# Hybrid decoder block, dense expert gates: in every second quad of tokens ScalarE builds the weighted table of first keys by itself

## The chip, the cores and the metric

The kernel runs on one core of one Trainium2 chip. The metric is device time in microseconds (us) of one execution. The engines are named as in the profile: PE is TensorE (PEld its weight loads), DVE is VectorE, ACT is ScalarE, POOL is GpSimd, SP is SyncE. Each engine works through its own instructions in order; engines wait for each other through semaphores.

## The reference, cut to what matters

One decoder layer on 1024 tokens of width 1024: a mixer (sliding-window attention and a gated convolution between an input and an output projection), and then a PEER layer, in which each token picks 128 of 16384 small experts (8 heads, 16 each). An expert's number is idx = e1 * 128 + e2, from two halves of the key search, and each has a gate:

```python
sc, ci = lax.top_k(cand, PEER_TOPK)
e1 = jnp.take_along_axis(i1, ci // PEER_TOPK, axis=-1)
e2 = jnp.take_along_axis(i2, ci % PEER_TOPK, axis=-1)
idx = e1 * N_KEYS + e2
gates = jax.nn.softmax(sc, axis=-1).astype(h.dtype)
...
a = jax.nn.gelu(jnp.einsum('td,thkd->thk', hx, u), approximate=False)
return jnp.einsum('thk,thkd->td', gx * a, vsel)
```

## The kernel before

The 1024 tokens are 8 tiles of 128. Three tiles (2, 6, 7) are "sparse": their experts' rows are gathered from memory one by one (POOL issues the gathers, DVE does the dot products, L970, and the sums, L977). Five tiles (0, 1, 3, 4, 5) are "dense": for them every expert is computed by matrix products (L1122 and L1168), and the result is weighted with a full matrix G of gates, one number for each expert and token, nearly all of them zero.

G is what the change is about. It is made in dense_gates1, one tile after the other, in quads of four tokens (32 quads to a tile, 160 in all; 8 quads fill one staging tile stg, which a DMA then writes to memory as part of G_d). For one token the 128 chosen experts lie on the partitions. Two tables of 128 x 128 are needed: oh2 has a one in each row at the column of e2, and og has the gate in each row at the column of e1. PE multiplies them (L846, four tokens to a quad), which gives the 128 x 128 gates of that token, and ACT copies the four from the PSUM bank G to stg (L847).

Before the change, DVE makes both tables of a quad in one is_equal against the row of numbers 0 to 127 in keyno (L823, 128 x 1024), with ones in both. Then the first one is multiplied with the gates: in quads 2 and 5 of each eight by ACT, token by token (L832, four instructions), in the other six by POOL in one instruction (L836). The tables oh have three buffers, so DVE can begin a quad when PE has done the one three before it.

All this runs beside the rest. The mixer and the key search are a "front" that runs three times (g0: tiles 0 to 2, g1: tiles 3 to 5, g2: tiles 6 and 7): input projection (lin_g1in), attention and convolution, output projection (lin_g1o), norm, query projection and key search (lin_g1q, pkg). Its weights come by DMA (raw), are split by ACT into a high part H (L223) and by POOL into a low part L (L224), and PE multiplies both (L268). The gates of tiles 0 and 1 are made beside front g1, those of tiles 3, 4 and 5 beside front g2, and a first part of the gathers of sparse tile 2 beside both. A counter in the program sets how many quads belong to each step of the front (gates_of.run); what is left by the end of g1's output projection is finished there (gates_of.rest). Up to the end of front g2 the order on each engine is then set by a scheduler at build time, which goes by its own estimates; the order is fixed when the kernel runs. The dense products behind it have an order written out by hand.

In names such as oh_1_40 the first number is the tile and the second the first token of the quad; G1_1_2 is the bank of tile 1, staging tile 1, quad 2. eT and gT hold e1, e2 and the gates of a tile, transposed.

Of the kernel before, what the change touches and what calls it, by code (L numbers as in the profile page):

```python
# [9 lines left out]
F32 = mybir.dt.float32  # L10
# [4 lines left out]
AF = mybir.ActivationFunctionType  # L15
ALU = mybir.AluOpType
PSUM = bass.MemoryType.PSUM

P = 128
# [4 lines left out]
NK = 128  # L24
# [60 lines left out]
def block_kernel(  # L85
# [18 lines left out]
    nc = tc.nc  # L104
# [48 lines left out]
    with ExitStack() as fctx:  # L153
# [14 lines left out]
        def bank(which, name):  # L168
            return (ps_a if which == "a" else ps_t).tile([P, 512], F32, tag="b", name=name)
# [20 lines left out]
        for i in range(7):  # L190
            pt = bank("t", f"selT_ps{i}")
# [6 lines left out]
        iota = fs.tile([P, NK], F32, name="iota")  # L198
        nc.gpsimd.iota(
            iota, pattern=[[1, NK]], base=0, channel_multiplier=0, allow_small_or_imprecise_dtypes=True  # L200
# [601 lines left out]
        def dense_gates(gg, tiles):  # L802
            for i in tiles:
                yield from dense_gates1(gg, i)

        def dense_gates1(gg, i):
            e1, e2 = yield from select(i)
            pt = bank("t", f"eT{i}")
            for k, s in enumerate((e1, e2, gates[i])):
                nc.tensor.transpose(pt[:, k * P : (k + 1) * P], s, ident)  # L810
            eT = gg.tile([P, 2, P], BF16, tag="eT", name=f"eT{i}", bufs=1)
            gT = gg.tile([P, P], F32, tag="gT", name=f"gT{i}", bufs=1)
            nc.scalar.copy(eT.rearrange("p a b -> p (a b)"), pt[:, : 2 * P])
            nc.scalar.copy(gT, pt[:, 2 * P : 3 * P])
            tg0 = DENSE.index(i) * (P // TG)
            pend = []
            for tg in range(P // TG):
                stg = gg.tile([P, NK, TG], F32, tag="stg", name=f"stg{i}_{tg}", bufs=2)
                for q in range(TG // 4):
                    t0 = tg * TG + q * 4  # L820

                    oh = gg.tile([P, 2, 4, NK], F32, tag="oh", name=f"oh_{i}_{t0}", bufs=3)
                    nc.vector.tensor_tensor(  # L823
                        oh,
                        keyno.unsqueeze(1).unsqueeze(1).to_broadcast([P, 2, 4, NK]),
                        eT[:, :, t0 : t0 + 4].unsqueeze(3).to_broadcast([P, 2, 4, NK]),
                        op=ALU.is_equal,
                    )
                    og, oh2 = oh[:, 0], oh[:, 1]
                    if q % 3 == 2:  # L830
                        for k in range(4):
                            nc.scalar.activation(  # L832
                                og[:, k, :], og[:, k, :], AF.Copy, scale=gT[:, t0 + k : t0 + k + 1]
                            )
                    else:
                        nc.gpsimd.tensor_tensor(  # L836
                            og, og, gT[:, t0 : t0 + 4].unsqueeze(2).to_broadcast([P, 4, NK]), op=ALU.mult
                        )
                    if pend:
                        pend.pop()()  # L840

                    def matmuls(oh2=oh2, og=og, stg=stg, tg=tg, q=q):

                        ps = bank("t", f"G{i}_{tg}_{q}").rearrange("p (e t) -> p e t", t=4)
                        for k in range(4):
                            nc.tensor.matmul(ps[:, :, k], oh2[:, k, :], og[:, k, :], start=True, stop=True)  # L846
                        nc.scalar.copy(stg[:, :, q * 4 : q * 4 + 4], ps)  # L847
                        if q == TG // 4 - 1:
                            nc.scalar.dma_start(
                                G_d.rearrange("b p g f -> p g b f")[:, tg0 + tg],  # L850
                                stg.rearrange("p (b e) t -> p b (e t)", e=GB),
                            )

                    pend.append(matmuls)
                    yield 1.2
            pend.pop()()
# [163 lines left out]
        keyno = ps_i.tile([P, 512], F32, name="keyno")[:, :NK]  # L1020
        nc.scalar.copy(keyno, iota)
        gg = fctx.enter_context(tc.tile_pool(name="gg", bufs=1, reuse_waits="tile", side="right"))
# [375 lines left out]
```

## Time and profile before

| | us |
|---|---|
| median of 3 runs (2874.75 to 2879.05) | 2877.15 |
| the profiled execution, whole | 2879.28 |
| its span, first to last instruction | 2877.2 |
| from 0 to 366: before the first quad's tables | 366 |
| 366 to 624: gates of tiles 0 and 1 beside front g1 | 258 |
| 624 to 740: key search of g1, input norm of g2, no gates | 116 |
| 740 to 1015: gates of tiles 3, 4 and 5 beside front g2 | 275 |
| 1100 to 2877: dense experts and the other gathers | 1777 |

The times in the left column are counted from the first instruction of the span. A table of stretches gives for each engine how long it was busy in each; an engine whose busy time equals the stretch has nothing left to give there.

### The profile page before, as it was taken

What the parts mean: (1) busy time and instruction counts of PE and PEld (TensorE: products, weight loads), DVE (VectorE), ACT (ScalarE), POOL (GpSimd) and SP (SyncE); (2) the same over time, 40 slices, a digit from 0 to 9 for tenths busy, and PEclk for the clock granted to TensorE, in tenths of its full rate; (3) what the DMA queues carried; (4) which work ended last, traced back from release to release, by engine and by line L of the source; (5) the groups of instructions that cost most, each with busy time, mean ns of one, the idle gap of its engine ahead of it and who ended that gap; (6) DMA issues with size and microseconds to landing.
All of it is one profiled execution on the core that took longest, in us unless ns stands there. A gap on an engine that the chain in (4) does not pass through costs nothing.

```text
span 2877.2 us, 43985 instructions
## 1 busy us (share of the span) xinstructions
PE 2667.0 (93%) x15358; PEld 2429.5 (84%) x15358; DVE 2215.0 (77%) x4645; ACT 1034.2 (36%) x2219; POOL 1907.3 (66%) x1894
## 2 busy tenths in 40 slices
PE   5998888988799778999999999999999999999997
PEld 4888866888678777999999889999999899999996
DVE  8826996869976877877777777777778777777776
ACT  3445445564466532222222322222222322222222
POOL 2445755657555756777777677777777777777771
PEclk9999898898899999999999999999999999999999
DMA  8635257773456757898988898898988889898884
GB/s 313 216 105 166 89 139 212 227 195 99 108 142 167 208 162 266 312 328 323 344 320 323 304 337 325 322 334 315 337 323 320 323 330 338 311 339 322 318 325 148
DMA packets 381978, 750.61 MB, mean 261 GB/s; under 512 B 188598, under 2 KB 194742, under 8 KB 381756
## 3 DMA queue, kind: packets, MB, share of 16 engines
q0 software_dynamic: 110592, 402.70, 38.0%
q1 hardware_dynamic: 107004, 303.16, 30.5%
q10 hardware_dynamic: 164160, 41.94, 6.8%
q8 instruction: 120, 1.97, 0.3%
q14 instruction: 102, 0.84, 0.1%
HBM read 695.79 MB, written 51.92 MB: 260 GB/s over the span
## 4 chain that ended last, share of the span: by engine, by line
PE 63%; DVE 5%; DMA 1%; ACT 1%; POOL 1%; issue 1%; another core or an unknown queue 0%; SPq 0%; DVEq 0%; ACTq 0%; POOLq 0%
PE A L1122 29%; PE V L1168 28%; PE G L846 2%; DVE oh L823 1%; PE lin_g2in L268 1%; PE lin_g2q L268 1%; DMA xr<-x1d 1%; PE lin_g2o L268 1%; DVE u L970 1%; DVE eq L728 0%; DMA V<-in_peer_v_dram 0%; POOL L L224 0%; DMA Gb<-G_d 0%; DVE eq L724 0%; DVE eq L717 0%
## 5 line engine op out<-in xcount | busy, mean ns | idle before, releaser
L949 POOL DMA_INDIRECT u<-in_peer_u_dram,idx x384 | 365.5, 952 | 235.0 <-DVE u L970 83.4
L224 POOL TENSOR_TENSOR L<-raw,H 128x512 fp32r<-128x512 f32 x252 | 335.4, 1343 | 273.7 <-ACT H L223 176.3
L1168 PE MATMUL V<-VH,WH 128*128 128x512 f32 x1280 | 503.0, 393 | 12.7 <-DVE acc_d L1175 9.6
L949 POOL DMA_INDIRECT v<-in_peer_v_dram,idx x384 | 363.4, 946 | 208.5 <-DVE u L970 67.7
L1168 PE MATMUL V<-VL,WH 128*128 128x512 f32 x1280 | 500.7, 391 | 0.0
L977 DVE SCALAR_TENSOR_TENSOR acc<-v,wv,acc 128x1024 f32<-128x1024 f32 x381 | 489.7, 1285 | 13.1 <-DMA v<-in_peer_v_dram,idx 7.5
L1168 PE MATMUL V<-VH,WL 128*128 128x512 f32 x1280 | 499.7, 390 | 0.0
L1127 ACT ACTIVATE A<-A 128x384 f32<-128x384 f32 (+1 forms) x256 | 107.7, 422 | 990.3 <-PE A L1122 750.9
L970 DVE SCALAR_TENSOR_TENSOR u<-u,h 128x1024 f32<-128x1024 f32 x384 | 457.7, 1214 | 2.8 <-DMA u<-in_peer_u_dram,idx 2.6
L1122 PE MATMUL A<-hDH,UH 128*128 128x384 f32 (+1 forms) x2048 | 344.5, 311 | 20.5 <-ACT UH L1085 19.2
L1105 POOL TENSOR_TENSOR VL<-V,VH 128x512 fp32r<-128x512 f32 x256 | 331.6, 1308 | 34.8 <-ACT VH L1101 32.4
L1122 PE MATMUL A<-hDH,UL 128*128 128x384 f32 (+1 forms) x2048 | 343.3, 310 | 9.8 <-POOL UL L1089 9.8
L1122 PEld LDWEIGHTS A<-hDH,UH 128*128 128x128 f32 x2048 | 321.1, 190 | 31.2 <-ACT UH L1085 20.0
L1139 DVE TENSOR_TENSOR A<-A,Gb 128x384 f32<-128x384 f32 (+1 forms) x256 | 126.4, 498 | 281.2 <-ACT A L1127 214.3
L1122 PE MATMUL A<-hDL,UH 128*128 128x384 f32 (+1 forms) x2048 | 341.3, 309 | 0.0
L1089 POOL TENSOR_TENSOR UL<-U,UH 128x1024 fp32r<-128x1024 f32 x128 | 308.7, 2412 | 33.2 <-ACT UH L1085 31.0
L1122 PEld LDWEIGHTS A<-hDH,UL 128*128 128x128 f32 x2048 | 311.6, 189 | 10.9 <-POOL UL L1089 10.9
L1122 PEld LDWEIGHTS A<-hDL,UH 128*128 128x128 f32 x2048 | 311.0, 189 | 0.0
L1168 PEld LDWEIGHTS V<-VH,WH 128*128 128x128 f32 x1280 | 241.7, 189 | 62.9 <-DVE acc_d L1175 13.8
L1168 PEld LDWEIGHTS V<-VH,WL 128*128 128x128 f32 x1280 | 241.6, 189 | 51.7
L1168 PEld LDWEIGHTS V<-VL,WH 128*128 128x128 f32 x1280 | 241.7, 189 | 45.1
L1175 DVE TENSOR_TENSOR acc_d<-acc_d,V 128x512 f32<-128x512 f32 x310 | 211.9, 684 | 55.0 <-PE V L1168 53.0
(313 smaller groups left out, 4324.0 us busy)
## 6 DMA issues: line engine op xcount, KB each, us to landing
U<-in_peer_uT_dram SPq DMA_DIRECT2D x128, 512.0 KB
V<-in_peer_v_dram SPq DMA_DIRECT2D x256, 256.0 KB
G_d<-stg ACTq DMA_DIRECT2D x20, 2048.0 KB
Gb<-G_d SPq DMA_DIRECT2D x64, 640.0 KB
raw<-in_w_in_dram SPq DMA_DIRECT2D x54, 512.0 KB
wada<-in_w_ada_dram SPq DMA_DIRECT2D x48, 512.0 KB
raw<-in_w_query_dram SPq DMA_DIRECT2D x48, 512.0 KB
raw<-in_w_out_dram SPq DMA_DIRECT2D x24, 512.0 KB
```

Of the source, the lines that this page charges most:

```text
L224: nc.gpsimd.tensor_tensor(L, src, H.bitcast(F32), op=ALU.subtract)
L268: nc.tensor.matmul(ps[:, :w], wt[:, c, :], h[:, q * (NC // 2) + c, o : o + w], start=(k == 0), stop=(k == 3 * NC - 1),)
L949: nc.gpsimd.indirect_dma_start(out=t, out_offset=None, in_=peer_u if which == "u" else peer_v, in_offset=bass.IndirectOffsetOnAxis(ap=idx[ ...
L970: nc.vector.scalar_tensor_tensor(t, t, 1.0, h2[i], op0=ALU.mult, op1=ALU.mult, accum_out=av[i][:, j : j + 1])
L977: nc.vector.scalar_tensor_tensor(acc[i], t, wv[i][:, j : j + 1], acc[i], op0=ALU.mult, op1=ALU.add)
L1089: nc.gpsimd.tensor_tensor(L, Ur.pop(b), Up[b][0].bitcast(F32), op=ALU.subtract)
L1105: nc.gpsimd.tensor_tensor(L, Vr.pop(v), Vp[v][0].bitcast(F32), op=ALU.subtract)
L1122: nc.tensor.matmul(ps[:, : n * P], u[:, c, :], h[:, c, sl], start=(k == 0), stop=(k == 3 * NC - 1))
L1127: nc.scalar.activation(w, w, AF.Gelu)
L1139: nc.vector.tensor_tensor(w3, w3, g, op=ALU.mult)
L1168: nc.tensor.matmul(ps, w[:, ts_], v, start=(n == 0), stop=(n == 3 * CB - 1))
L1175: nc.vector.tensor_tensor(accs[0][:, t, hs], accs[0][:, t, hs], ps, op=ALU.add)
```

## The change

In every odd quad of each eight (1, 3, 5, 7) DVE makes the table of e2 alone (128 x 512), and ACT makes the weighted table of e1 from nothing but the numbers 0 to 127 (iota) and one column each of the gates and of two negated copies (ng: of e1 and of the gates): first Abs(number - e1), then Relu(gate - gate * that), which is the gate where the number is e1 and zero elsewhere, since the distance is otherwise at least one. Each is an instruction per token, so eight per quad. In every even quad DVE makes both tables as before and POOL multiplies. So 80 quads go through ACT where 40 did, and 80 through POOL where 120 did. The two negated copies are made once for each tile.

```diff
@@ -812,6 +812,9 @@
             gT = gg.tile([P, P], F32, tag="gT", name=f"gT{i}", bufs=1)
             nc.scalar.copy(eT.rearrange("p a b -> p (a b)"), pt[:, : 2 * P])
             nc.scalar.copy(gT, pt[:, 2 * P : 3 * P])
+            ng = gg.tile([P, 2, P], F32, tag="ng", name=f"ng{i}", bufs=1)
+            nc.scalar.activation(ng[:, 0], pt[:, 0:P], AF.Copy, scale=-1.0)
+            nc.scalar.activation(ng[:, 1], pt[:, 2 * P : 3 * P], AF.Copy, scale=-1.0)
             tg0 = DENSE.index(i) * (P // TG)
             pend = []
             for tg in range(P // TG):
@@ -820,19 +823,28 @@
                     t0 = tg * TG + q * 4
 
                     oh = gg.tile([P, 2, 4, NK], F32, tag="oh", name=f"oh_{i}_{t0}", bufs=3)
-                    nc.vector.tensor_tensor(
-                        oh,
-                        keyno.unsqueeze(1).unsqueeze(1).to_broadcast([P, 2, 4, NK]),
-                        eT[:, :, t0 : t0 + 4].unsqueeze(3).to_broadcast([P, 2, 4, NK]),
-                        op=ALU.is_equal,
-                    )
                     og, oh2 = oh[:, 0], oh[:, 1]
-                    if q % 3 == 2:
+                    if q % 2:
+                        nc.vector.tensor_tensor(
+                            oh2,
+                            keyno.unsqueeze(1).to_broadcast([P, 4, NK]),
+                            eT[:, 1, t0 : t0 + 4].unsqueeze(2).to_broadcast([P, 4, NK]),
+                            op=ALU.is_equal,
+                        )
+
                         for k in range(4):
+                            t = t0 + k
+                            nc.scalar.activation(og[:, k, :], iota, AF.Abs, bias=ng[:, 0, t : t + 1])
                             nc.scalar.activation(
-                                og[:, k, :], og[:, k, :], AF.Copy, scale=gT[:, t0 + k : t0 + k + 1]
+                                og[:, k, :], og[:, k, :], AF.Relu, scale=ng[:, 1, t : t + 1], bias=gT[:, t : t + 1]
                             )
                     else:
+                        nc.vector.tensor_tensor(
+                            oh,
+                            keyno.unsqueeze(1).unsqueeze(1).to_broadcast([P, 2, 4, NK]),
+                            eT[:, :, t0 : t0 + 4].unsqueeze(3).to_broadcast([P, 2, 4, NK]),
+                            op=ALU.is_equal,
+                        )
                         nc.gpsimd.tensor_tensor(
                             og, og, gT[:, t0 : t0 + 4].unsqueeze(2).to_broadcast([P, 4, NK]), op=ALU.mult
                         )
```

How this moves the instructions, at one place on two engines: the output projection of front g1, beside the quads of tile 1. First ACT, before. L223 is the split of a weight, L588 and L574 belong to the projection's result, L847 empties a bank of G.

```order
L847 COPY stg1_1_5170<-G1_1_0_5184 128x128x4
L223 CAST H_64_0_5375<-raw_64_5373 128x512
L832 ACTIVATE oh_1_40_5245<-oh_1_40_5245,gT1_4964 128x128 x4
L588 ACTIVATE junk2g1_0_0_5203,ss8_g1_5124<-x1g1_5120 128x128
L223 CAST H_64_1_5379<-raw_64_5373 128x512
L588 ACTIVATE junk2g1_0_1_5205,ss8_g1_5124<-x1g1_5120 128x128
L588 ACTIVATE junk2g1_0_2_5207,ss8_g1_5124<-x1g1_5120 128x128
L847 COPY stg1_1_5170<-G1_1_1_5251 128x128x4
L574 ACTIVATE osg1_2_5290<-lin_g1o2_0_5301,gb_65,acol_62 128x384
L847 COPY stg1_1_5170<-G1_1_2_5260 128x128x4
L832 ACTIVATE oh_1_52_5326<-oh_1_52_5326,gT1_4964 128x128 x4
```

And ACT now, from the same bank on. L837 is the Abs, L838 the Relu, and L859 empties a bank of G.

```order
L859 COPY stg1_1_5286<-G1_1_0_5307 128x128x4
L859 COPY stg1_0_5061<-G1_0_7_5290 128x128x4
L837 ACTIVATE oh_1_44_5377<-iota_164,ng1_5058 128x128 x4
L588 ACTIVATE junk2g1_0_0_5326,ss8_g1_5233<-x1g1_5229 128x128
L223 CAST H_64_0_5513<-raw_64_5511 128x512
L861 DMA G_d_84<-stg1_0_5061 128x64x64
L838 ACTIVATE oh_1_44_5377<-oh_1_44_5377,gT1_5055,ng1_5058 128x128
L223 CAST H_64_1_5517<-raw_64_5511 128x512
L838 ACTIVATE oh_1_44_5377<-oh_1_44_5377,gT1_5055,ng1_5058 128x128
L574 ACTIVATE osg1_2_5417<-lin_g1o2_0_5428,gb_65,acol_62 128x384
L838 ACTIVATE oh_1_44_5377<-oh_1_44_5377,gT1_5055,ng1_5058 128x128 x2
L588 ACTIVATE junk2g1_0_1_5328,ss8_g1_5233<-x1g1_5229 128x128
```

Where ACT had one group of four instructions for two or three banks, it has now eight for each second bank, and the weight splits and the projection's results stand between them.

On PE, at the same place, before (L268 is the output projection, its third block):

```order
L846 MATMUL G1_1_2_5260<-oh_1_40_5245 128x128 x4
L268 MATMUL lin_g1o3_0_5383<-hDH_68,H_63_0_5293 128x384 x3
L268 MATMUL lin_g1o3_0_5383<-hDL_69,H_63_0_5293 128x384 x4
L268 MATMUL lin_g1o3_0_5383<-hDH_68,L_63_0_5294 128x384 x4
L846 MATMUL G1_1_3_5269<-oh_1_44_5257 128x128 x4
L579 MATMUL oTg1_1_0_5279<-ident_97,osg1_1_5209 128x128 x3
L268 MATMUL lin_g1o3_0_5383<-hDH_68,H_63_1_5297 128x384 x4
```

And now:

```order
L858 MATMUL G1_1_2_5387<-oh_1_40_5368 128x128 x4
L268 MATMUL lin_g1o3_0_5521<-hDH_68,H_63_0_5420 128x384
L268 MATMUL lin_g1o3_0_5521<-hDL_69,H_63_0_5420 128x384 x4
L268 MATMUL lin_g1o3_0_5521<-hDH_68,L_63_0_5421 128x384 x4
L268 MATMUL lin_g1o3_0_5521<-hDH_68,H_63_1_5424 128x384 x4
L858 MATMUL G1_1_3_5396<-oh_1_44_5377 128x128
L268 MATMUL lin_g1o3_0_5521<-hDL_69,H_63_1_5424 128x384 x4
L268 MATMUL lin_g1o3_0_5521<-hDH_68,L_63_1_5425 128x384 x2
L858 MATMUL G1_1_3_5396<-oh_1_44_5377 128x128
L268 MATMUL lin_g1o3_0_5521<-hDH_68,L_63_1_5425 128x384 x2
L268 MATMUL lin_g1o4_0_5602<-hDH_68,H_64_0_5513 128x384
L858 MATMUL G1_1_3_5396<-oh_1_44_5377 128x128
```

The four products of an odd quad (G1_1_3) stood together; now they stand one by one between those of the projection, as each token's table is due.

## Rows read from the trace of the kernel before

**Rows 1.** Part 1 of the page: busy time, share of span, instructions.

```profile
PE 2667.0 (93%) x15358; PEld 2429.5 (84%) x15358; DVE 2215.0 (77%) x4645; ACT 1034.2 (36%) x2219; POOL 1907.3 (66%) x1894
```

**Rows 2.** Stretches, columns: start:end, length, busy of PE, PEld, DVE, ACT, POOL.

```profile
366.00:1015.00 649.00, 553.07 (x3556) 503.45 (x3556) 521.02 (x1451) 350.78 (x837) 391.35 (x472) 0.91 0.61 167
624.00:740.00 116.00, 96.77 (x606) 94.63 (x605) 110.94 (x639) 46.73 (x97) 78.03 (x167) 0.91 0.41 118
1100.00:2877.00 1777.00, 1744.37 (x9744) 1586.28 (x9744) 1363.98 (x1995) 485.45 (x954) 1300.17 (x1097) 0.99 0.87 318
```

**Rows 3.** Groups by line, 366 to 1015: busy, mean ns | idle before, releasers.

```profile
L823 DVE TENSOR_TENSOR oh<-keyno,eT 128x1024 f32<-128x1024 f32 x160 | 191.5, 1217 | 57.2 <-PE G L846 51.1 <-POOL L L224 4.0 <-ACT eT L813 1.6
...
L846 PE MATMUL G<-oh 128*128 128x128 f32 x1280 | 190.0, 303 | 45.6 <-POOL oh L836 40.8 <-ACT oh L832 4.6
...
L224 POOL TENSOR_TENSOR L<-raw,H 128x512 fp32r<-128x512 f32 x143 | 189.5, 1336 | 94.5 <-ACT H L223 75.2 <-PE lin_g1in L268 7.5 <-PE lin_g1q L268 3.3
...
L836 POOL TENSOR_TENSOR oh<-oh,gT 128x512 f32<-128x512 f32 x120 | 130.2, 1087 | 111.1 <-DVE oh L823 108.7 <-PE pT L414 1.4 <-PE lin_g2o L268 0.3
...
L847 ACT COPY stg<-G 128x512 f32<-128x512 f32 x160 | 91.9, 584 | 87.2 <-PE G L846 86.9
...
L832 ACT ACTIVATE oh<-oh,gT 128x128 f32<-128x128 f32 x160 | 51.7, 395 | 30.7 <-DVE oh L823 30.4
```

**Rows 4.** Seven stretches with gates, all engines.

```profile
366.00:400.00 34.00, 24.78 (x151) 21.96 (x150) 34.00 (x65) 15.90 (x41) 16.96 (x14) 0.90 0.43 104
530.00:552.00 22.00, 17.31 (x83) 15.37 (x84) 21.63 (x30) 8.40 (x20) 16.08 (x16) 0.69 0.75 226
552.00:602.00 50.00, 46.65 (x333) 46.37 (x332) 30.65 (x34) 38.58 (x115) 35.03 (x31) 1.00 0.75 196
740.00:770.00 30.00, 21.19 (x133) 19.84 (x133) 29.90 (x40) 12.44 (x29) 20.23 (x16) 0.78 0.29 84
770.00:800.00 30.00, 22.62 (x153) 18.66 (x151) 26.78 (x48) 18.90 (x52) 14.40 (x13) 0.99 0.71 149
835.00:875.00 40.00, 37.02 (x246) 33.96 (x245) 37.78 (x69) 19.85 (x43) 21.27 (x18) 0.87 0.50 141
875.00:950.00 75.00, 62.48 (x498) 59.58 (x497) 47.70 (x50) 53.06 (x141) 50.36 (x46) 0.96 0.72 179
```

**Rows 5.** The same stretches, line 823 alone (x is quads begun).

```profile
366.00:400.00 34.00, 17.74 (x15) 0.90 0.43 104
530.00:552.00 22.00, 10.62 (x9) 0.69 0.75 226
552.00:602.00 50.00, 25.35 (x21) 1.00 0.75 196
740.00:770.00 30.00, 12.62 (x11) 0.78 0.29 84
770.00:800.00 30.00, 19.37 (x17) 0.99 0.71 149
835.00:875.00 40.00, 14.46 (x13) 0.87 0.50 141
875.00:950.00 75.00, 43.90 (x37) 0.96 0.72 179
```

**Rows 6.** Timeline of ACT: one quad's four gate multiplications, start and length.

```profile
561.58 1.28 ACT L832 ACTIVATE oh<-oh,gT 128x128 f32<-128x128 f32 x4 [0.67 <-DVE oh L823]
```

**Rows 7.** Groups on ACT, 366 to 1015: two column operands, and none.

```profile
L298 ACT ACTIVATE stg_x<-nT_g2a,acol,A 128x256 f32<-128x256 f32 x8 | 4.4, 577 | 0.0
...
L629 ACT COPY qqsg<-lin_g2q 128x256 f32<-128x256 f32 x10 | 3.8, 376 | 1.1 <-PE lin_g2q L268 1.1
```

**Rows 8.** Page, part 5: a 128x512 operation of DVE with one PSUM input.

```profile
L1175 DVE TENSOR_TENSOR acc_d<-acc_d,V 128x512 f32<-128x512 f32 x310 | 211.9, 684 | 55.0 <-PE V L1168 53.0
```

**Rows 9.** Groups on ACT, 366 to 1015: loads of a function table.

```profile
L935 ACT ACT_TABLE_LOAD x3 | 3.8, 1283 | 0.1
```

## The prediction, made before the changed kernel ran

> **What bounds the kernel now.** I read the busy times first: PE is busy 93% of the span, DVE 77%, POOL 66%, ACT 36% [rows 1]. By that list ACT is the engine with room. But the change touches only the stretch in which gates are made, and a share of the whole span says nothing of it, so I cut it out. From 1100 on PE is busy 1744 of 1777 us and no gate is made there; the change leaves that part alone. From 366 to 1015 us, without the 116 us in the middle that hold no gates, there are 533 us, and in these PE is busy 553.1 - 96.8 = 456 (86%), DVE 521.0 - 110.9 = 410 (77%), ACT 350.8 - 46.7 = 304 (57%), POOL 391.4 - 78.0 = 313 (59%) [rows 2]. So no engine is full there on average. What the gates cost is seen in the idle times of their groups: PE sits 45.6 us idle in front of the products of G, nearly all of it until POOL has multiplied a table; POOL waits 108.7 us for DVE's tables; and DVE waits 51.1 us for PE to give a buffer back [rows 3]. It is a ring of DVE, POOL and PE with three buffers.
>
> The average hides two kinds of stretches [rows 4]. In some DVE is full: 34.0 of 34 us from 366 to 400, 21.6 of 22 from 530 to 552, 29.9 of 30 from 740 to 770, 37.8 of 40 from 835 to 875 (key search, gathers and selection run there beside the gates). In three others DVE has room, and ACT is already at 38.6 of 50 us (552 to 602), 18.9 of 30 (770 to 800) and 53.1 of 75 (875 to 950), since the projections' weight splits and results run on ACT there. The quads begun in each are counted by the rows of line 823 [rows 5].
>
> **What the change removes.** DVE: in 80 quads a table of 512 columns takes the place of one of 1024. The long one takes 1217 ns [rows 3]. No such short one is in the trace; the nearest row is another operation of DVE on 128x512 numbers with one input in PSUM, 684 ns [rows 8], so 533 ns are saved per odd quad, 43 us of busy time in all. POOL loses 40 multiplications of 1087 ns, 43 us. ACT loses its 160 old ones, 51.7 us, that is 0.323 us averaged over the 160 quads [rows 3].
>
> **What it adds: an odd quad on ACT.** Four Abs and four Relu on 128x128. The Abs has one column operand, like the old multiplication: 395 ns, and a run of four takes 1.28 us [rows 3, 6], so each further one costs (1.28 - 0.395)/3 = 0.295. The Relu has two, a scale and a bias. What a column operand costs is seen between two groups of 128x256 numbers out of PSUM: 577 ns with two, 376 without, so 100 each [rows 7]; a Relu is then 0.495 alone and 0.395 in a run. Together 4 x 0.295 + 4 x 0.395 = 2.76, and about 0.1 for the joint where a Relu needs an Abs to have ended and can't overlap it: 2.85 us. From below it is eight times 0.295, 2.4; from above eight lone instructions, 4 x 0.395 + 4 x 0.495 = 3.6. I take 2.85, since the new order on ACT keeps most of them in fours. 80 x 2.85 = 228 us against 52 taken away: ACT gets 176 us more in the 533, and would stand at 304 + 176 = 480, 90%. That is above what PE, the fullest engine there, has now. No share of an average proves a bound, so I do the sum by stretches, each as old ACT time - 0.323 x quads + 2.85 x quads/2 [rows 4, 5]:
> 366 to 400: 15.9 - 4.8 + 21.4 = 32.4 of 34. 530 to 552: 18.3 of 22. 740 to 770: 24.6 of 30. 835 to 875: 34.2 of 40. These still fit.
> 552 to 602: 38.6 - 6.8 + 29.9 = 61.7 of 50, 11.7 over. 770 to 800: 18.9 - 5.5 + 24.2 = 37.6 of 30, 7.6 over. 875 to 950: 53.1 - 12.0 + 52.7 = 93.8 of 75, 18.8 over.
> The three are **38 us** over. The added work can't be put off: the same queue holds the splits of the weights, which POOL already awaits for 75.2 us [rows 3], the results of the projections, and the copies that give PSUM banks back, so PE stands when ACT lags. The new order shows them standing between the Relus.
>
> **What is gained.** Where DVE is full, 0.533 us for each odd quad would shorten the stretch at most: 15 + 9 + 11 + 13 = 48 quads [rows 5], 24 odd ones, 12.8 us. I take 6, since in these stretches an odd quad's product now comes after 2.85 us of ACT, where it came after 1.2 on DVE and 1.1 on POOL, and ACT has little room in the first and the last of them. POOL's 43 us lie beside other engines' work: it is busy 59% there, and none of the seven stretches has it over three quarters full; at nothing, therefore. If that is wrong, PE's wait for POOL, 40.8 us [rows 3], falls by the third of POOL's quads that go away, 13.6 us.
>
> **Small things.** Two copies for each of five tiles, about 0.3 us each, 3 us of ACT. The order has two loads of a function table more than before (a GELU of the gathers falls between attention's exponentials once more), 1.3 us each [rows 9]. Half of these 6 us on the path: 3.
>
> **The sum.** 38 - 6 + 3 = +35 us. The profiled execution took 2879.3, so it would take 2914; against the median of 2877.15 that is 2912. I say 2913.
>
> A page of the Trainium skill speaks to this. Perfetto Trace Analysis, section Optimizing Scalar/DVE Operations, says that with DVE saturated it may make sense to offload work to Scalar, and also that grouping into larger operations improves throughput where the engine is saturated. The two pull apart here: the first speaks for the change and would end near the faster rival below, while by the second eight operations of 128 columns are the wrong form for an engine that they fill. The trace agrees with the first for 126 us of the seven stretches and has DVE with room in the other 155.
>
> **Rivals.**
> *ACT's overflow is absorbed* (faster, 2857). The overflow goes into the free ACT time beside the full stretches (5 us before 770, 6 before 875, 4 before 552), the Abs needs no table from DVE and can run early, and the ring becomes shorter on DVE and POOL: up to 12.8 + 13.6 = 26 us less; less the 6 of small things, 2857. For it speaks that PE's idle time in front of G goes to POOL for 40.8 us and to ACT for 4.6 [rows 3]. Against it: three buffers let ACT run ahead by one or two odd quads only, and 15 us of room against 38 of overflow. It decides if an odd quad costs ACT under 2 us. Chance 0.14.
> *A draw* (2872 to 2883): half the overflow absorbed and DVE's gain in full, 19 - 13 = 6 us at most. Chance 0.09.
> *ACT becomes the gate of the whole front* (2950). An engine on which others wait, and that waits for them, is not full even when it bounds: PE, which bounds these stretches now, is busy 46.7 of 50, 22.6 of 30 and 62.5 of 75 [rows 4], that is 93, 75 and 83%. If ACT gets no fuller than that, they last 61.7/0.93 = 66, 37.6/0.75 = 50 and 93.8/0.83 = 113 us: 16 + 20 + 38 = 74 us more, 2951. Chance 0.2.
> *The change does not do what it says*: the order shows the eight instructions and the short table in every odd quad, so this has no chance worth a number.
>
> **How the numbers follow.** ACT as the bound at about the size of the sum: chance 0.57; as the gate of the whole front 0.2; a draw 0.09; faster 0.14. About 0.2%, 6 us, is what a measurement of this kernel can tell from no change. So slower 0.77, same 0.09, faster 0.14. The range has to hold the draw and most of the gate: 2866 to 2950 leaves out the better part of the faster case and the worst of the gate, 0.2 together.
>
> **What would show it.** Right: ACT's busy time up by some 180 us, an odd quad at 2.6 to 3.1 us, ACT over 90% busy where the output projections of g1 and g2 run, these stretches longer, PE idle in front of G until ACT rather than POOL, and waits for H (L223) up. DVE down by 43 us and POOL too, with nothing of it in the end. The part behind the front lasts as long as before. Wrong: if the two output projections take no longer than before while ACT is fuller, the overflow found room, and the sum fails at the step where it adds up the three stretches. If Relu costs no more than Abs, an odd quad is 2.4 us and the overflow falls by some 17 us, to about 21. If PE stands longer in the stretches in which DVE is full, my gain of 6 us has the wrong sign.

## The result and the profile after

The changed kernel takes 2922.7 us (median of 4 runs, 2914.4 to 2928.3), the kernel before, run beside it, 2876.0 (2874.4 to 2879.1): a ratio of 1.016, with a 95% interval of 1.0145 to 1.0174. That is 47 us slower, where 36 were forecast, and inside the range. The profiled execution is the quickest of the four, 2914.4 us with a span of 2912.6; the working below goes by its 35 us.

Part 1 and a row of part 2 of the page after (busy time and share; tenths of 40 slices of 72.8 us):

```profile
PE 2680.7 (92%) x15358; PEld 2437.5 (84%) x15358; DVE 2167.3 (74%) x4645; ACT 1193.2 (41%) x2711; POOL 1863.8 (64%) x1854
...
ACT  3445476874778943222222222222222222222222
```

Against [rows 1] DVE has 48 us less, POOL 44 less, ACT 159 more. All three went where they were meant to go, and yet the time rose. Over the whole span ACT is still the least busy engine. In the slices in which gates are made (the sixth to the fourteenth) it is at six to nine tenths, but for the tenth, the key search of g1.

The groups of the gates, from 366 to 1055 us of the kernel after (busy, mean ns | idle before, releasers), answer to [rows 3]:

```profile
L858 PE MATMUL G<-oh 128*128 128x128 f32 x1273 | 203.6, 312 | 65.8 <-ACT oh L838 39.3 <-POOL oh L848 22.4 <-DVE oh L828 1.7
...
L224 POOL TENSOR_TENSOR L<-raw,H 128x512 fp32r<-128x512 f32 x144 | 190.7, 1337 | 118.1 <-ACT H L223 89.2 <-PE lin_g2in L268 10.5 <-PE lin_g1o L268 4.5
...
L838 ACT ACTIVATE oh<-oh,gT,ng 128x128 f32<-128x128 f32 x316 | 137.7, 498 | 0.0
...
L837 ACT ACTIVATE oh<-iota,ng 128x128 f32<-128x128 f32 x316 | 103.0, 404 | 0.0
...
L842 DVE TENSOR_TENSOR oh<-keyno,eT 128x1024 f32<-128x1024 f32 x78 | 95.1, 1220 | 91.4 <-PE G L858 79.2 <-ACT pTs L418 7.8 <-ACT eT L813 2.4
...
L828 DVE TENSOR_TENSOR oh<-keyno,eT 128x512 f32<-128x512 f32 x79 | 53.9, 682 | 11.4 <-PE G L858 11.0
```

PE's wait in front of G is now first of all for ACT's Relu (L838), 39.3 us, where it was for POOL, 40.8, and for ACT only 4.6; 22.4 us of the wait for POOL are left. ACT itself never waits in front of Abs or Relu: the idle time there is 0.0. The copies that give PSUM banks back (L847, now L859) still wait for PE, but for 37.3 us where it was 86.9. By these rows an odd quad costs ACT (137.7 + 103.0)/79 = 3.05 us, the short table DVE 682 ns.

Where the time went is seen best when the span is cut at the first and last products of each step on PE. This table is worked out from the start times of the groups lin_g1in, lin_g1q, lin_g2in, A and of the transposes of the norms; kernels that come later stand beside it, each as its difference to the kernel before, from its own profiled execution.

| step, us | before | after | e1 | e2 | e4 | e5 | e7 | e8 | e6 |
|---|---|---|---|---|---|---|---|---|---|
| to the first product of g1 | 322.9 | -4.8 | -2.4 | -0.8 | +1.4 | -3.2 | -1.3 | -1.4 | -2.9 |
| g1 input projection, attention (tile 0) | 190.4 | +1.6 | +3.8 | -1.9 | +1.7 | -3.4 | -8.9 | -6.0 | +16.0 |
| g1 output projection to its norm (tile 1) | 91.7 | +5.0 | -3.1 | +3.7 | -0.7 | +3.0 | -1.8 | -6.9 | +20.3 |
| g1 key search | 88.0 | 0.0 | +0.1 | +0.4 | +0.4 | +0.4 | +1.5 | +0.4 | +1.0 |
| g2 input projection, attention (tile 3, start of 4) | 175.4 | +8.8 | +7.3 | -4.3 | +10.4 | -2.9 | -9.0 | -15.1 | +30.2 |
| g2 output projection to its norm (tiles 4, 5) | 82.8 | +23.1 | +3.4 | +21.2 | +10.1 | +2.1 | -1.7 | -2.8 | +41.4 |
| g2 key search (end of tile 5) | 85.9 | +4.5 | +1.2 | +1.0 | -2.2 | -0.4 | +3.2 | +1.4 | -1.7 |
| dense experts | 1840.1 | -2.8 | +1.7 | +1.9 | +4.0 | +1.8 | -3.9 | +1.4 | -2.6 |

The part without gates is the same to within 5 us in each. The loss lies beside g2's output projection above all, then in g2's input phase, then beside g1's output projection. The same stretches of the kernel after, with its own times (start:end, length, busy of PE, PEld, DVE, ACT, POOL, then the granted clock):

```profile
510.00:607.00 97.00, 79.43 (x472) 69.55 (x471) 52.12 (x77) 84.43 (x241) 45.17 (x40) 0.89 0.60 169
770.00:800.00 30.00, 21.60 (x125) 19.09 (x125) 17.89 (x38) 28.58 (x84) 7.65 (x7) 0.79 0.67 141
879.00:985.00 106.00, 84.94 (x549) 77.01 (x547) 50.28 (x73) 93.53 (x265) 44.67 (x39) 0.84 0.60 151
```

ACT is the busiest engine in all three: 87, 95 and 88%. DVE, relieved, is at 54, 60 and 47%. In the last of them the chain of waits runs through ACT from 941 to 958 us with hardly a break; the latter part of it (start, length, what):

```profile
951.40 0.29 ACT junk2g L588 x2
951.98 1.73 ACT oh L838 x4
953.71 0.29 ACT junk2g L588 x2
954.00 0.47 ACT stg L859
954.47 1.18 ACT oh L837 x4
955.65 0.29 ACT junk2g L588 x2
955.95 0.95 ACT stg L859 x2
956.89 0.89 ACT oh L837 x3
957.78 0.40 ACT oh L838
958.22 0.79 PE G L858 x2
```

L588 belongs to the output projection. It stands in one queue with the Abs, the Relu and the copies of G, as the order had shown, and the norm behind the projection waits for the last of them. The chain can be followed back to 940.6 us; of its 44 us up to the norm, 11 are PE's (from 958.2 to 965.2 and from 974.7 to 978.5 above all) and nearly all others ACT's. Over the same step of the kernel before, the chain is PE's first of all: 35.3% products of G, 22.2% of the projection.

### The profile page after: what moved, and what is told of

It reads as the page before. It is cut to its first block, busy times and chain, and to the rows that moved or that the text cites. A ratio compares the mean times of both kernels' runs of the same rounds, so it can differ in the third digit from the quotient of the medians.

```text
span 2912.6 us, 44410 instructions
## 1 busy us (share of the span) xinstructions
PE 2680.7 (92%) x15358; PEld 2437.5 (84%) x15358; DVE 2167.3 (74%) x4645; ACT 1193.2 (41%) x2711; POOL 1863.8 (64%) x1854
## 4 chain that ended last, share of the span: by engine, by line
PE 59%; DVE 4%; ACT 2%; DMA 1%; POOL 1%; issue 1%; SPq 0%; DVEq 0%; POOLq 0%; ACTq 0%
PE A L1134 29%; PE V L1180 28%; DMA xr<-x1d 0%; PE G L858 0%; ACT oh L838 0%; DVE eq L728 0%; PE lin_g2q L268 0%; ACT oh L837 0%; DMA Gb<-G_d 0%; DMA raw<-in_w_query_dram 0%; POOL UL L1101 0%; POOL u L961 0%; DVE eq L724 0%; POOL L L224 0%; DVE eq L717 0%
```

## The experiments

Theory A is the prediction's: ACT's throughput is the bound where the projections' own work already runs on it. Rival B is that an odd quad costs its share anywhere, because its table comes late in the ring of three buffers. Rival C is that the new order costs by itself.

**The scheme in two tiles, and in the other three (e1, e2).** The tiles are 0 and 3 in e1 and (1, 4, 5) in e2; where the scheme is off, ACT multiplies in quads 2 and 5, as before.

```diff
+FULL = (0, 3)
...
-                    if q % 2:
+                    if i in FULL and q % 2:
```

> The new scheme only in tiles 0 and 3, whose quads run mostly beside the input projections and attention; tiles 1, 4 and 5 as in the kernel before. Theory A (ACT is overfull where the output projections run): most of the loss is beside the output projections of g1 and g2, so it is gone here; what is left is the lengthening of g2's input phase, about 9 us: 2876 to 2890 us. Rival B (every odd quad costs its share wherever it runs, because its table comes late in the ring of three buffers): 64 of 160 quads, 40% of 47 us: 2895.

Measured: 2892.7 us, ratio 1.0058 (1.0037 to 1.0079), 16 us slower. That is 3 us above A's range and 2 below B's value, so the total tells them badly apart, and rather for B. The table of steps does better: beside g2's output projection 3 of the 23 us are left, beside g1's the time is 3 us below the kernel before. What is left sits in g1's and g2's input phases, +4 and +7 us.

> The complement: the new scheme only in tiles 1, 4 and 5, tiles 0 and 3 as before. Theory A: the loss beside the output projections stays, 5 us in g1 and 23 to 28 in g2, so 2904 to 2912. Rival B: 96 of 160 quads, 60% of 47: 2904. The two differ in the stretches: by A the time from the start of g2's output projection to its norm is 20 us or more above the kernel before, and g2's input phase is as before.

Measured: 2903.1 us, ratio 1.0091 (1.0074 to 1.0108), 27 us slower: 1 us below A's range, and at B's 2904. By steps g2's output projection takes 21 us more, g1's 4, and the input phases are 2 and 4 us shorter than before. The two losses, 16 and 27, make 43 of the 47 us, so they add up. Per odd quad they are alike, 16/32 = 0.51 and 27/48 = 0.56 us, which is what B says of the totals. By steps a quad's cost depends on where it runs, as A says, but the input phases cost more than I had expected of them under A.

**Work taken off ACT, and put on DVE (e4).**

```diff
-                        nc.scalar.copy(stg[:, :, q * 4 : q * 4 + 4], ps)
+                        if q % 2:
+                            nc.vector.tensor_copy(stg[:, :, q * 4 : q * 4 + 4], ps)
+                        else:
+                            nc.scalar.copy(stg[:, :, q * 4 : q * 4 + 4], ps)
```

> The changed kernel, but DVE instead of ACT empties the bank of G in every odd quad: 80 copies of 584 ns leave ACT (47 us), 80 of about 690 ns come to DVE (55 us). Theory A: ACT is the bound beside the output projections, DVE has room there; 20 to 35 of the 47 us come back: 2888 to 2903. Rival B (the ring, which DVE leads): DVE's queue gets longer and the ring slower, so 2923 or more.

Measured: 2903.3 us, ratio 1.0085 (1.0068 to 1.0102); 19.5 us of the 47 come back, half a us short of what A expected, and B's value is missed by 20: DVE got 54.9 us more and the kernel became faster.

```profile
L860 DVE COPY stg<-G 128x512 f32<-128x512 f32 x80 | 54.9, 686 | 46.2 <-PE G L858 45.7
```

The gain lies where DVE had room: 13 us beside g2's output projection (23.1 to 10.1) and 6 beside g1's. In g2's input phase, where DVE is full for a part of the time, nothing is gained.

**Half the quads (e5).** ACT builds the table in quads 1 and 5 of each eight, POOL multiplies in the other six.

```diff
-                    if q % 2:
+                    if q % 4 == 1:
```

> ACT makes the weighted table in two quads of each eight instead of four; POOL multiplies in the other six, as many as in the kernel before. Theory A: ACT gets 40 x 3.05 = 122 us where it had 52 before and 241 after, which fits into every stretch, and DVE keeps half its gain: 2868 to 2882. Rival B: half the loss stays: 2899.

Measured: 2877.5 us, ratio 1.0000 (0.9991 to 1.0010). Inside A's range, 21 us from B's value. Half the scheme costs nothing where the whole costs 47: the cost is not in proportion to the quads. By steps the input phases gain 3 us each and the output projections lose 3 and 2.

**The dose (e8, e7, e6).** The same kernel with other amounts of work for ACT in an odd quad. e8 leaves out Abs and Relu and multiplies a constant table, e7 leaves out the Relu; both leave out the gates of the odd quads. e6 does the Abs twice. The three edits, e6, e7 and e8 (fixed is a tile of zeros, made once for each tile of tokens):

```diff
+                            nc.scalar.activation(og[:, k, :], iota, AF.Abs, bias=ng[:, 0, t : t + 1])
                             nc.scalar.activation(og[:, k, :], iota, AF.Abs, bias=ng[:, 0, t : t + 1])
                             nc.scalar.activation(
                                 og[:, k, :], og[:, k, :], AF.Relu, scale=ng[:, 1, t : t + 1], bias=gT[:, t : t + 1]
                             )
```

```diff
                             nc.scalar.activation(og[:, k, :], iota, AF.Abs, bias=ng[:, 0, t : t + 1])
-                            nc.scalar.activation(
-                                og[:, k, :], og[:, k, :], AF.Relu, scale=ng[:, 1, t : t + 1], bias=gT[:, t : t + 1]
-                            )
```

```diff
-                    og, oh2 = oh[:, 0], oh[:, 1]
+                    og, oh2 = (fixed if q % 2 else oh[:, 0]), oh[:, 1]
```

> The changed kernel without Abs and Relu; PE multiplies a constant table in odd quads, so their gates are left out and the output is not the reference's. It shows what the short table and the relief of POOL and ACT are worth at most: DVE has 43 us less, POOL 43, ACT 52 less than the kernel before. Prediction's bound for these gains: 13 to 26 us, so 2850 to 2863 us by theory A; with the 6 us that I took, 2870.

> The changed kernel without the Relu, so an odd quad costs ACT 1.28 us where it cost 3.05; leaves out the weighting with the gates in odd quads, so the output is not the reference's. Theory A: 102 us of ACT where the kernel before had 52, which fits everywhere; the loss goes, and half or more of what DVE gained is left: 2862 to 2878 us. Rival C (the new order on PE and ACT costs by itself, whatever ACT's load): 2895 or more, since the products stay scattered.

> The changed kernel with each Abs of an odd quad done twice (same output): four more instructions per odd quad, 1.18 us, 94 us of ACT in all, and not one more on DVE, POOL or PE. Theory A (ACT's throughput): beside g2's output projection 18 odd quads add 22 us to an engine 88% busy, so that phase lasts some 25 us longer, g1's 12 to 14 longer, g2's input phase 10 to 20 longer: 2970 to 2985 us. Rival B (the ring's latency; ACT has air): only the delay of a table counts, and where other work covers it nothing: 2925 to 2945.

| | ACT per odd quad, us | time, us | ratio to before (95% interval) |
|---|---|---|---|
| e8 | 0 | 2849.8 | 0.9903 (0.9884 to 0.9923) |
| e7 | 103.5/80 = 1.29 | 2859.4 | 0.9949 (0.9932 to 0.9967) |
| after | 3.05 | 2922.7 | 1.016 (1.0145 to 1.0174) |
| e6 | (140.0 + 108.3 + 105.1)/80 = 4.42 | 2982.1 | 1.0372 (1.0355 to 1.0390) |

The rows for e6 (both lines of Abs, the Relu, and PE's products), 340 to 1150 us:

```profile
L839 ACT ACTIVATE oh<-oh,gT,ng 128x128 f32<-128x128 f32 x320 | 140.0, 499 | 0.0
...
L838 ACT ACTIVATE oh<-iota,ng 128x128 f32<-128x128 f32 x320 | 108.3, 406 | 0.0
...
L837 ACT ACTIVATE oh<-iota,ng 128x128 f32<-128x128 f32 x320 | 105.1, 406 | 0.0
...
L859 PE MATMUL G<-oh 128*128 128x128 f32 x1280 | 222.1, 330 | 117.7 <-ACT oh L839 91.1 <-POOL oh L849 17.1 <-ACT stg L860 4.1
```

And those for e7 (the Abs, and PE's products):

```profile
L837 ACT ACTIVATE oh<-iota,ng 128x128 f32<-128x128 f32 x320 | 103.5, 399 | 0.0
...
L855 PE MATMUL G<-oh 128*128 128x128 f32 x1280 | 180.3, 295 | 35.1 <-POOL oh L845 21.0 <-DVE oh L828 9.4 <-ACT oh L837 2.3
```

The first 1.29 us cost 10 us over 80 quads, 0.09 for each us of ACT's time; the next 1.76 cost 63, or 0.45; the last 1.37 cost 59, or 0.54. ACT's busy time in part 1 of the pages, in which two instructions that overlap count once, is 989.3 us in e8, 1077.3 in e7, 1193.2 after and 1281.9 in e6: by it the steps are 88, 116 and 89 us, at 0.11, 0.55 and 0.67 for each. That is how an engine comes out that first has room and then is the bound in a growing part of the stretches. A table that comes late in the ring could show a knee too, so this series alone does not part A from B; the steps of e1 and e2, and e4, do so beside the output projections. PE's wait for ACT's table in front of G goes with it, 2.3, 39.3 and 91.1 us. e6 adds nothing to DVE, POOL or PE and lands in A's range and 37 us above B's. e7 and e8 lie 3 us and less below A's ranges. C was to be tried by e7, but e7 does not try it: its order is not the scattered one. On PE the product of a token is two matmuls, that of a quad eight. Unbroken series of them that do not hold whole quads are 7 in the trace of the kernel before, 61 after, but only 14 in e7. What speaks against C is e4, with 68 such series and 19.5 us less than the kernel after, and e6, with 52 and 59 us more: the time follows ACT's load and not the scatter. What share of the 63 us between e7 and after the scattered order has by itself is not shown.

**Which relief is worth something (h1), and a version from it.** The kernel before with the gate multiplication on ACT in four quads of eight; no short table.

```diff
-                    if q % 3 == 2:
+                    if q % 2:
```

> The kernel before with one number changed: ACT multiplies the table with the gates in every odd quad (4 of 8) instead of quads 2 and 5; DVE makes both tables everywhere, as before. ACT does 80 x 1.28 us for odd quads, as in e7_abs_only, and POOL 80 multiplications, as there; only DVE's short table is missing. If DVE's relief is what e7 and e8 gained by: 2870 to 2878 us, no gain. If POOL's relief is: 2858 to 2866, and this version beats both kernels.

Measured: 2875.9 us beside 2880.1 for the kernel before, ratio 0.9988 (0.9979 to 0.9997). ACT's 102.5 us and POOL's 80 multiplications are those of e7. What is missing is DVE's short table, and one thing more that goes with it: e7's Abs needs no table from DVE, while h1's multiplication waits for one.

```profile
L832 ACT ACTIVATE oh<-oh,gT 128x128 f32<-128x128 f32 x320 | 102.5, 393 | 42.0 <-DVE oh L823 40.9 <-ACT stg L847 0.9
```

e7 gains 2874.6 - 2859.4 = 15 us on the kernel before that ran beside it, h1 4, so at this load of ACT the short table and ACT's independence of DVE are worth 11 us together; how much is the one and how much the other was not tried. h1 itself is 0.12% faster, less than the 0.2% that I count as clear.

**Half the quads in tiles 0 and 3 alone (f1).**

```diff
-                    if q % 2:
+                    if i in FULL and q % 4 == 1:
```

> A version that may beat both: in tiles 0 and 3 alone, ACT makes the weighted table in quads 1 and 5 of each eight; the other tiles as in the kernel before. Theory A: 16 quads of tiles 0 and 3 save DVE 0.53 us each where DVE is full and ACT has room, nothing is added beside the output projections: 2868 to 2874 us. If the input phases don't gain, 2874 to 2878.

Measured: 2875.0 us, ratio 1.0001 (0.9991 to 1.0011). No gain: g1's input phase is 3 us shorter, g2's 2 us longer. No version of the whole computation that was run beats the kernel before by a clear margin; a way to make the weighted table with one instruction per token on ACT, which e7's time would reward, I did not find. The ring with a fourth buffer was not tried.

## Why the prediction was right

**The bound.** ACT turned into it beside both output projections: the steps of e1, e2 and e4 and the chain of waits show it there. From 770 to 800 us, the third place, it is 95% busy, but in g2's input phase as a whole it is not shown whether ACT's throughput costs the time or a table that comes late in the ring: PE waits 13.8 us there for POOL's tables and 11.7 for ACT's (699 to 879), and e4, which takes copies off ACT and gives them to DVE, gains nothing there. The rival of an absorbed overflow is out, and so is the draw. The rival in which ACT is the gate of the whole front lies 28 us away, the sum 10.

**An odd quad on ACT.** Forecast 2.85 us, measured 3.05 by the groups: the Abs 404 ns and the Relu 498 alone (forecast 395 and 495), and fewer of them stand in unbroken fours than I took. The groups count twice what an instruction overlaps with its neighbour of another line: four Abs that begin at 784.53 us of the kernel after last 1.29 us, and the Relu behind them begins at 785.71. By ACT's busy time in part 1 of the pages, 1193.2 us after and 989.3 in e8, an odd quad costs 203.9/80 = 2.55 us. So the 0.1 us that the forecast added where a Relu follows an Abs is not seen, and by this count 2.85 was somewhat too high. The gap between 404 and 498, 94 ns, is the second column operand, which I had put at 100 from [rows 7]. The short table takes 682 ns (forecast 684).

**The overflow, 38 us, was too small a term.** e8 gives the size: without any Abs or Relu the kernel takes 2849.8, with them 2922.7, so what ACT does in odd quads costs 73 us. The sum counts from a kernel in which ACT still has its 52 us of old multiplications; at the 0.09 of e7's first step these are worth some 5 us, so in the sum's terms it is about 68 (an estimate from e7 and e8), where overflow and small things made 41. In part this is because the sum assumed that ACT is full wherever it is the bound. It is 87 and 88% busy beside the output projections (84.4 of 97, 93.5 of 106 us), and 93% in e6 (115.0 of 124). But by steps most of it lies elsewhere. From e8 to the kernel after, which are 64 us apart in their profiled executions, g1's output projection grows by 11.9 us (forecast 11.7), g2's by 25.9 (18.8), g2's input phase by 23.9 (7.6) and g1's by 7.6 (nothing). Some 24 us are missing in the input phases, most of which the sum took to have room. Its seven stretches hold 281 of the 533 us and 123 of the 160 quads; in the kernel after ACT is busy 43.9 of the 50 us from 400 to 450, which none of the seven covers, and 113.6 of the 139 us from 740 to 879. This is the step that was mis-sized most. The rival that put ACT at PE's own shares came to 74, but not by place: it has 38 us beside g2's output projection and nothing in g1's input phase.

**The gain, 6 us, was too small as well.** With ACT lightly loaded DVE's short table, together with ACT's independence of DVE, is worth 11 us (e7 against h1), where I took 6 of a ceiling of 12.8; POOL's relief, taken together with ACT's 51 us of added multiplications, comes to 4 (h1), where I had set it at nothing. e8, which has everything that the change takes off DVE, POOL and ACT and none of what it puts on ACT, is 25 us faster than the kernel before, about 20 without the 5 for ACT's old multiplications; the 10 us between it and e7 go with the first 1.29 us per quad of ACT. What I had against the gain, that ACT's longer path to a table eats it up, was not measured by itself.

Both errors nearly cancel: 68 - 20 = 48 stands beside 41 - 6 = 35. That the forecast fell as near the time as it did is luck in this part.

**The places.** Forecast 11.7 us beside g1's output projection, 7.6 in the stretch from 770 to 800 and 18.8 beside g2's, before any gain; measured, all gains included, +5.0 and +23.1 beside the two projections and +8.8 in g2's whole input phase. The forecast that DVE's relief shortens the input phases did not show in the total: e7 has them 9 us shorter each, the kernel after, with more work on ACT, 1.6 and 8.8 longer. The stretch from 770 to 800 was counted among those in which DVE has room, though DVE was busy 26.8 of its 30 us [rows 4]. In g2's input phase PE is idle 45.5 of 180 us where it was idle 35.6 of 171 before, so by the prediction's own sign the gain of 6 us did not come there. And the 9 us are not all DVE's: h1, cut into the same steps, has g1's input phase 8.1 us shorter with DVE's long table, and only g2's (1.4 shorter) falls behind e7.

**The signs.** DVE down by 48 us and POOL by 44 (43 each), PE's wait in front of G now ACT's first of all, waits for H up from 75.2 to 89.2, the dense part unchanged: all as written down. ACT's busy time went up by 159 us, less than the 180 of the forecast. ACT over 90% busy beside the output projections is not what came: 87 and 88%.

The Trainium skill, in Perfetto Trace Analysis, section Optimizing Scalar/DVE Operations, says that offloading from a saturated DVE to Scalar may make sense. The runs agree with it by half: e7 against h1 puts DVE's relief, with ACT's independence of it, at 11 us, and e4 shows work going back from ACT to DVE for a gain of 19.5. The engine from which work should go is not the same in each stretch.

## What to carry to other kernels

Cut the time to the stretch in which the moved work runs before calling an engine free: ACT was 36% busy over the span, 57% over the stretches with gates, and over 70% in the one that lost most. Add up the receiving engine's new load stretch by stretch, over all stretches, and allow for its not being full where it is the bound (87 to 93% here) and for a cost where the sum finds little or none (32 us in the two input phases here, from e8 to the kernel after, where 7.6 were forecast). And look for the knee: half of the move cost nothing, the whole of it 47 us, so a dose series of three kernels tells more than one trial.

## What was not expected of the hardware

PE's granted clock fell where PE came to wait for ACT, and its own work grew longer with it. Beside g2's output projection the clock is 0.94 before, 0.84 after and 0.82 in e6:

```profile
868.00:951.00 83.00, 69.48 (x536) 65.79 (x535) 54.24 (x63) 56.16 (x147) 52.38 (x47) 0.94 0.70 175
```

```profile
933.00:1057.00 124.00, 87.18 (x542) 78.30 (x540) 48.90 (x72) 114.96 (x339) 43.48 (x38) 0.82 0.51 131
```

The first fence is the kernel before, the second e6. About the same number of products kept PE busy for 69.5 us before, 84.9 after and 87.2 in e6; a matmul of G took 303, 312 and 330 ns on average over all gates. The clock has two levels, 2.4 and 1.2 GHz, so 0.84 means about a third of that stretch at the lower one. The clock does not account for all of it: 69.5 x 0.94/0.84 is 78 us and not 84.9, and at the same clock of 0.92 PE is busy 70.4 us there in e8 and 77.9 in e4. How much of this lay on the path, and not beside ACT's work, was not settled.
